# Three settings of a hybrid decoder trunk: which feed-forward chunks use seven products, when a norm is summed, and which engine splits six weight pieces

## The chip, the cores and the metric

The kernel runs on one core of one Trainium2 chip. The metric is the device time of one execution in microseconds (us). The engines are named as in the profile: PE (TensorE), PEld (its weight loads), DVE (VectorE), ACT (ScalarE), POOL (GpSimd) and SP (SyncE, whose queue issues the weight transfers).

## The reference, cut to what matters

A trunk of two layers works on 512 tokens of 1024 features in float32. Each layer has a mixer and then a SwiGLU feed-forward network of 2816 hidden features; layer 0 mixes by attention (a latent group and a differential group), layer 1 by two recurrences.

```python
def swiglu(h, w_gate, w_up, w_down):
    return (jax.nn.silu(h @ w_gate) * (h @ w_up)) @ w_down
...
    x = x + m
    x = x + swiglu(rms_norm(x, norm_ffn[l]), ffn_gate[l], ffn_up[l], ffn_down[l])
```

In the latent group of layer 0 the keys and values come from a normed projection of 256 features:

```python
    kv = (rms_norm(c_kv, kv_norm) @ w_ukv).reshape(bsz, s_len, MLA_HEADS, MLA_NOPE + MLA_V).transpose(0, 2, 1, 3)
```

## The kernel before, in words

**Split products.** Every float32 operand is split into a high and a low part in a format that PE multiplies in one pass; a product of two operands is then three matmuls (`mm3`, L362 to L364): high by high, low by high, high by low. Activations are held as features by tokens in eight tiles of 128x512.

**Weights.** They come from HBM in groups of 512 KB, four of which are held at a time (`NRAW`), and are cut into pieces of 128x512. `cut_one` casts a piece to its high part `wh` on ACT (L300) and subtracts it from the raw weight to get the low part `wl` (L302). The subtraction runs on GpSimd for the pieces numbered `PL[0]` up to `PL[1]`, and on DVE otherwise. The pieces are numbered in the order of use: 0 to 7 are the first projections, 8 to 15 the differential values, 16 to 23 the differential queries and keys of heads 2 and 3, 24 onwards the latent projections. Cutting runs at most eight pieces ahead of use (`NSPL`).

**Steps.** A dense step is one 128x128 weight tile with its three matmuls of 512 columns. After each step `tick` counts one, runs what is due, and may cut a piece. `defer(n, f)` runs `f` n steps later. Instructions go into each engine's queue about in this order, and each queue is worked off in order.

**The feed-forward network.** `ffn` goes through the hidden features in two halves of 11 chunks of 128. A plain chunk has 16 steps, eight for the gate (`pg`) and eight for the up product (`pu`); `gated` then reads both from PSUM (L1092 on DVE, L1093 on ACT, L1094 on DVE, L1095 on GpSimd) and splits the hidden tile (L1096, L1097). PSUM has three banks of the tag `mm` for these: the up product of chunk 3 takes the bank in which the gate product of chunk 2 was. The chunks in `FAST[half]` are computed by `seven` as a Strassen product of 2x2 blocks: seven products of 12 matmuls with 256 columns each (L1054), which need four sums of weights (`combined`, L322 to L330, two on GpSimd and two on DVE) and seven pieces instead of four. They also need four pairs of sums of activations, the same for all such chunks; `halves(j)` makes one pair: two products by the norm's weights on ACT (L1029), four sums on DVE (L1031 to L1034), two casts on ACT (L502) and two subtractions on DVE (L503). Each pair is deferred from the start of chunk 0. The norm's row (`rstd`, L473 to L484) and what is done with chunk 0 come at step 21 (`W0` is 5).

**The latent norm.** In layer 0 a weave of two generators puts attention blocks of the differential heads between dense steps. In `latent_projections`, j counts six tiles of eight steps. The squares of the two key tiles (j of 1 and 2) are added on GpSimd (L517); `scale_kv` sums them over the features with eight matmuls of one column (L683) and takes the root (L687 to L690); `spread_kv` lays the result out over the tokens (L696), loads two tables through SP's queue and turns the shared key (L707 to L711). `SK` gives the steps, counted from j of 3 and j of 4, behind which these two run:

```python
hooks = {3 + SK[0] // 8: {SK[0] % 8: scale_kv}, 4 + SK[1] // 8: {SK[1] % 8: spread_kv}}
```

Of the kernel before, what the change touches and what calls it, by code (L numbers as in the profile page):

```python
# [39 lines left out]
R0, R1 = 8, 12  # L40
W0 = 5
SQ = 2, 6
SK = 2, 0
PT = 2
PL = 16, 72
KP = 4
NW = 16
Z0, Z1 = 3, 9
# [10 lines left out]
HC = lambda nc: nc.scalar.copy  # L59
NSLOT, NTMP, NRAW, NSPL = 38, 10, 4, 8  # L60

FAST = (4, 6, 8, 10), (0, 2, 4, 6, 8, 10)
SEVEN = "a11", "s2", "s1", "a22", "s3", "a12", "s4"


# [117 lines left out]
def drain(gen):  # L183
    for _ in gen:
        pass


class Build:
    def __init__(self, nc, tc, a, ctx, dbg=None):
# [10 lines left out]
        for key, c, src, total, width in self.weight_order():  # L200
            self.chunks[key, c] = len(self.pieces), width
            size = width if key == "first" else 2 * width
            if key[:2] == "gu" and c % HFF in FAST[c // HFF]:
                n = len(self.groups)
# [78 lines left out]
    def cut_one(self):  # L283
# [17 lines left out]
        if lo is not None:  # L301
            (nc.gpsimd if PL[0] <= self.cut < PL[1] else nc.vector).tensor_tensor(out=lo, in0=raw, in1=hi.bitcast(F32), op=ALU.subtract)  # L302
        self.have[self.cut] = hi, lo
# [362 lines left out]
    def latent_projections(self):  # L666
# [56 lines left out]

        hooks = {3 + SK[0] // 8: {SK[0] % 8: scale_kv}, 4 + SK[1] // 8: {SK[1] % 8: spread_kv}}
        for c in range(3):
# [288 lines left out]
    def ffn(self, l, wcol):  # L1014
# [9 lines left out]
        def halves(j):  # L1024

            tt = nc.vector.tensor_tensor
            a, b, s = self.tmp("xa"), self.tmp("xb"), (self.tmp("b12"), self.tmp("b34"))
            for t, k in ((a, j), (b, j + 4)):
                nc.scalar.activation(out=t, in_=self.x[:, k, :], func=AF.Identity, scale=self.par[:, own + k : own + k + 1])  # L1029
            la, lb = slice(0, 256), slice(256, T)  # L1030
            tt(out=s[0][:, la], in0=a[:, lb], in1=a[:, la], op=ALU.subtract)  # L1031
            tt(out=s[0][:, lb], in0=b[:, lb], in1=s[0][:, la], op=ALU.subtract)
            tt(out=s[1][:, la], in0=b[:, lb], in1=a[:, lb], op=ALU.subtract)
            tt(out=s[1][:, lb], in0=s[0][:, lb], in1=b[:, la], op=ALU.subtract)  # L1034
            for i in range(2):
                self.split(mixed[j][0][i], mixed[j][1][i], s[i])

        for half in range(2):
# [50 lines left out]
            def gated(pg, pu, row):  # L1089
                g, u = self.tmp("g"), self.tmp("uu")  # L1090
                h, lo = self.slot("hh", F32R), self.slot("hl", F32R)
                nc.vector.tensor_tensor(out=g, in0=pg, in1=row, op=ALU.mult)  # L1092
                nc.scalar.activation(out=g, in_=g, func=AF.Silu)  # L1093
                nc.vector.tensor_tensor(out=u, in0=pu, in1=row, op=ALU.mult)  # L1094
                nc.gpsimd.tensor_tensor(out=u, in0=u, in1=g, op=ALU.mult)  # L1095
                nc.scalar.copy(out=h, in_=u)  # L1096
                nc.gpsimd.tensor_tensor(out=lo, in0=u, in1=h.bitcast(F32), op=ALU.subtract)  # L1097
                hh.append(h)
                hl.append(lo)

            for m in range(HFF):
                w = self.weights(f"gu{l}", half * HFF + m)
                if half == m == 0:
                    for j in range(KD // 2):
                        self.defer(22 + 7 * j, lambda j=j: halves(j))
                    row = self.first_tiles(w, gated, None, squares)
                    continue
                if m in FAST[half]:
                    seven(w)
                    continue  # L1110
                pg, pu = self.bank("mm"), self.bank("at" if half == 0 and m == 1 else "mm")
                drain(self.featmajor(pg, w, 0, self.ah, self.al))
                drain(self.featmajor(pu, w, 1, self.ah, self.al))
                gated(pg, pu, row)
# [604 lines left out]
```

## Time and profile before

| | us |
|---|---|
| median of 3 runs | 1277.98 (1276.56 to 1280.1) |
| profiled execution | 1278.92 |
| its span | 1277.1 |
| PE busy in it | 1245.8 |

In the profiled execution 1.82 us lie around the span. PE is busy for 98% of the span, and the mean granted clock of TensorE is 0.991 of full speed; a matmul's busy time overlaps with that of the next, so that a stretch is timed by the starts of its matmuls, and an idle PE and a lowered clock are two separate losses.

### The profile page before, as it was taken

Reading aid. Unit: us, or ns where it says so; the run is one execution under the profiler, and the core shown is the slowest. Engines: PE = TensorE matmul, PEld = TensorE weight load, DVE = VectorE, ACT = ScalarE, POOL = GpSimd, SP = SyncE. Lnnn points to the kernel's source line nnn. Section 1 sums busy time; section 2 is a strip of 40 time slices with the busy share of each in tenths; the row PEclk is TensorE's granted clock in tenths of the full one; section 3 lists DMA queues with packets and bytes.
Section 4 is the critical chain, followed back from the end, with each engine's and each line's share of the span. In section 5 each row is a group of like instructions: output and inputs, shape, how many; then the busy total and the mean of one; then the engine's idle time right before and its main releaser. Section 6 shows DMA issues by size and latency. Waiting matters only on the chain.

```text
span 1277.1 us, 18331 instructions
## 1 busy us (share of the span) xinstructions
PE 1245.8 (98%) x6777; PEld 1060.1 (83%) x6777; DVE 845.5 (66%) x1583; ACT 603.4 (47%) x1235; POOL 349.7 (27%) x281
## 2 busy tenths in 40 slices
PE   9999999998999999999999999999989999999997
PEld 7877778876898889898888888777769888999886
DVE  7786676577785456774475466999877744676632
ACT  6555655556444234444433455564554432434441
POOL 0753431123442014331200013210044310335212
PEclk9999999999999999999999999999989999999999
DMA  7222221121323322333422420212313233233321
GB/s 260 87 87 62 83 83 50 34 66 50 100 89 114 110 87 97 101 98 99 130 71 82 133 92 23 70 47 66 94 56 100 79 114 105 85 114 91 107 68 66
DMA packets 38120, 113.37 MB, mean 89 GB/s; under 512 B 4368, under 2 KB 10896, under 8 KB 38032
## 3 DMA queue, kind: packets, MB, share of 16 engines
q1 hardware_dynamic: 37888, 111.95, 28.0%
q8 instruction: 53, 0.87, 0.3%
q14 instruction: 35, 0.29, 0.1%
q10 hardware_dynamic: 144, 0.26, 0.1%
HBM read 110.10 MB, written 2.10 MB: 88 GB/s over the span
## 4 chain that ended last, share of the span: by engine, by line
PE 82%; DVE 7%; ACT 3%; issue 2%; POOL 1%; POOLq 0%; ACTq 0%; DVEq 0%
PE mm L362 18%; PE mm L363 18%; PE mm L364 18%; PE mm L1054 14%; PE at L1054 2%; PE o L947 1%; PE at L781 1%; PE at L1511 1%; DVE bl L503 1%; PE at L903 1%; PE at L800 1%; DVE wl L302 1%; PE o L890 1%; ACT p L792 1%; DVE nm L788 1%
## 5 line engine op out<-in xcount | busy, mean ns | idle before, releaser
L302 DVE TENSOR_TENSOR wl<-wr,wh 128x512 fp32r<-128x512 f32 x332 | 272.7, 831 | 202.9 <-ACT wh L300 200.2
L300 ACT CAST wh<-wr 128x512 fp32r<-128x512 f32 (+1 forms) x385 | 229.7, 608 | 287.8 <-PE mm L363 201.2
L362 PE MATMUL mm<-xh,wh 128*128 128x512 f32 x608 | 242.2, 399 | 9.9 <-DVE g L1092 8.9
L364 PE MATMUL mm<-xh,wl 128*128 128x512 f32 x608 | 240.0, 395 | 0.4 <-POOL wl L302 0.4
L363 PE MATMUL mm<-xl,wh 128*128 128x512 f32 x608 | 239.4, 394 | 0.3 <-DVE xl L506 0.3
L362 PEld LDWEIGHTS mm<-xh,wh 128*128 128x128 f32 x608 | 115.6, 190 | 33.5 <-issue 6.2
L362 PE MATMUL mm<-hh,wh 128*128 128x512 f32 (+1 forms) x363 | 139.2, 383 | 0.0
L363 PE MATMUL mm<-hl,wh 128*128 128x512 f32 (+1 forms) x363 | 138.9, 383 | 0.0
L364 PE MATMUL mm<-hh,wl 128*128 128x512 f32 (+1 forms) x363 | 138.9, 383 | 0.0
L364 PEld LDWEIGHTS mm<-xh,wl 128*128 128x128 f32 x608 | 115.4, 190 | 25.3 <-POOL wl L302 0.9
L363 PEld LDWEIGHTS mm<-xl,wh 128*128 128x128 f32 x608 | 115.8, 190 | 23.3 <-DVE xl L506 0.7
L302 POOL TENSOR_TENSOR wl<-wr,wh 128x512 fp32r<-128x512 f32 (+1 forms) x54 | 69.2, 1288 | 110.3 <-ACT wh L300 103.7
L300 ACT CAST wh<-s 128x512 fp32r<-128x512 f32 x80 | 47.7, 617 | 97.1 <-DVE s L323 71.9
L1095 POOL TENSOR_TENSOR uu<-uu,g 128x512 f32<-128x512 f32 x24 | 42.3, 1764 | 146.4 <-ACT g L1093 68.4
L364 PEld LDWEIGHTS mm<-hh,wl 128*128 128x128 f32 x363 | 68.2, 188 | 13.4
L363 PEld LDWEIGHTS mm<-hl,wh 128*128 128x128 f32 x363 | 68.2, 188 | 13.2
L362 PEld LDWEIGHTS mm<-hh,wh 128*128 128x128 f32 x363 | 68.2, 188 | 13.1
L1083 POOL TENSOR_TENSOR uu<-uu,g 128x512 f32<-128x512 f32 x20 | 30.3, 1515 | 151.7 <-ACT g L1082 151.7
L1054 PE MATMUL mm<-bh,wh 128*128 128x256 f32 x240 | 68.3, 284 | 0.0
L1054 PE MATMUL mm<-xh,wl 128*128 128x256 f32 x240 | 67.9, 283 | 0.0
L1054 PE MATMUL mm<-xl,wh 128*128 128x256 f32 x240 | 67.9, 283 | 0.0
L1054 PE MATMUL mm<-bl,wh 128*128 128x256 f32 x240 | 67.9, 283 | 0.0
(465 smaller groups left out, 2695.4 us busy)
## 6 DMA issues: line engine op xcount, KB each, us to landing
wr<-in_w_gu_dram SPq DMA_DIRECT2D x88, 512.0 KB, 3.6
wr<-in_w_down_dram SPq DMA_DIRECT2D x32, 512.0 KB, 3.5
wr<-in_w_in_dram SPq DMA_DIRECT2D x18, 512.0 KB, 3.7
wr<-in_w_out_dram SPq DMA_DIRECT2D x12, 512.0 KB, 3.5
wr<-in_w_down_dram SPq DMA_DIRECT2D x32, 192.0 KB, 2.4
x<-in_x_dram SPq DMA_DIRECT2D x8, 256.0 KB, 5.8
wr<-in_w_dv_dram SPq DMA_DIRECT2D x4, 512.0 KB, 6.9
tab<-in_con_dram SPq DMA_DIRECT2D x8, 256.0 KB, 4.0
```

What stands on the lines that cost most here:

```text
L300: nc.scalar.copy(out=hi, in_=raw)
L302: (nc.gpsimd if PL[0] <= self.cut < PL[1] else nc.vector).tensor_tensor(out=lo, in0=raw, in1=hi.bitcast(F32), op=ALU.subtract)
L362: mm(out, lh, rh, start=start, stop=False)
L363: mm(out, lh, rl, start=False, stop=False)
L364: mm(out, ll, rh, start=False, stop=stop)
L503: nc.vector.tensor_tensor(out=lo, in0=src, in1=hi.bitcast(F32), op=ALU.subtract)
L781: nc.tensor.matmul(s[:, 0:n], qb, k[:, 0:n], start=True, stop=True)
L788: nc.vector.tensor_reduce(out=nm, in_=s[:, 0:n], axis=AX.X, op=ALU.max, negate=True)
L792: nc.scalar.activation(out=pt[:, 0:n], in_=s[:, 0:n], func=AF.Exp, bias=nm, accum_out=rsum)
L1054: mm = lambda x, y, a, b: nc.tensor.matmul(ps[:, la], x, y, start=a, stop=b, skip_group_check=True)
L1083: nc.gpsimd.tensor_tensor(out=u, in0=u, in1=g, op=ALU.mult)
L1095: nc.gpsimd.tensor_tensor(out=u, in0=u, in1=g, op=ALU.mult)
```

## The change

`FAST[0]`, the chunks of the first half that use seven products, becomes 5, 7 and 9 in place of 4, 6, 8 and 10, in both layers; the second half stays. The four pairs of sums of activations are deferred by 38, 47, 56 and 65 steps in place of 22, 29, 36 and 43. `scale_kv` and `spread_kv` run three dense steps later. Pieces 16 to 21 have their low part subtracted on DVE in place of GpSimd.

```diff
-SK = 2, 0
+SK = 5, 3
 PT = 2
-PL = 16, 72
+PL = 22, 72
...
-FAST = (4, 6, 8, 10), (0, 2, 4, 6, 8, 10)
+FAST = (5, 7, 9), (0, 2, 4, 6, 8, 10)
...
                 if half == m == 0:
                     for j in range(KD // 2):
-                        self.defer(22 + 7 * j, lambda j=j: halves(j))
+                        self.defer(38 + 9 * j, lambda j=j: halves(j))
```

## Rows read from the trace of the kernel before

**Rows 1.** The page's first part: busy us, share of span, instructions.

```profile
PE 1245.8 (98%) x6777; PEld 1060.1 (83%) x6777; DVE 845.5 (66%) x1583; ACT 603.4 (47%) x1235; POOL 349.7 (27%) x281
```

**Rows 2.** PE's waits by releaser: us in total, times, longest.

```profile
PE mm L362 <- DVE g L1092: 8.9, 2, 5.8
```

**Rows 3.** Windows of layer 0's chunks: length, PE, PEld, DVE, ACT, POOL busy, clock, DMA.

```profile
296.73:307.61 10.88, 10.88 (x49) 9.01 (x48) 10.26 (x19) 8.24 (x14) 4.77 (x3) 1.00 0.02 3
307.61:313.05 5.44, 5.44 (x25) 4.32 (x23) 3.08 (x5) 3.01 (x6) 4.81 (x4) 1.00 0.24 90
313.05:319.03 5.98, 0.16 (x1) 0.03 (x1) 5.98 (x11) 2.80 (x6) 0.94 (x1) 0.76 0.00 0
319.03:326.45 7.42, 7.42 (x25) 5.94 (x26) 6.31 (x7) 3.44 (x7) 3.15 (x2) 0.73 0.41 116
326.45:336.55 10.10, 10.10 (x86) 10.10 (x85) 7.24 (x10) 3.94 (x8) 6.30 (x4) 1.00 0.28 78
336.55:347.45 10.90, 10.90 (x51) 9.01 (x50) 8.12 (x14) 5.10 (x9) 2.90 (x2) 1.00 0.35 106
```

**Rows 4.** Windows of layer 1: chunk 3 between its two products, and its second.

```profile
943.58:948.96 5.38, 0.55 (x2) 0.19 (x2) 5.38 (x10) 3.10 (x7) 1.63 (x1) 0.88 0.00 0
948.96:957.09 8.13, 8.13 (x24) 6.51 (x25) 5.52 (x8) 3.34 (x7) 4.69 (x2) 0.66 0.37 129
```

**Rows 5.** Timeline of DVE in layer 0's chunks 2 and 3: start us, us.

```profile
306.36 0.41 DVE L1033 TENSOR_TENSOR b<-xb,xa 128x256 f32<-128x256 f32 x1
...
310.40 1.85 DVE L503 TENSOR_TENSOR bl<-b,bh 128x512 fp32r<-128x512 f32 x1 [2.36 <-ACT bh L502]
...
317.60 0.68 DVE L503 TENSOR_TENSOR bl<-b,bh 128x512 fp32r<-128x512 f32 x1
318.21 0.68 DVE L1092 TENSOR_TENSOR g<-mm,row 128x512 f32<-128x512 f32 x1
```

**Rows 6.** Timeline of POOL and ACT there.

```profile
305.65 3.55 POOL L1095 TENSOR_TENSOR uu<-uu,g 128x512 f32<-128x512 f32 x1 [5.38 <-ACT xa L1029]
...
309.23 0.62 ACT L1096 CAST hh<-uu 128x512 fp32r<-128x512 f32 x1 [2.98 <-POOL uu L1095]
```

**Rows 7.** Timeline of PE, POOL and DVE around pieces 16 to 23.

```profile
53.08 0.50 PE L364 MATMUL mm<-xh,wl 128*128 128x512 f32 x1 [0.43 <-POOL wl L302]
...
51.75 8.76 POOL L302 TENSOR_TENSOR wl<-wr,wh 128x512 fp32r<-128x512 f32 x7
...
56.69 3.85 DVE L918 SCALAR_TENSOR_TENSOR ri<-ri,nlam,rsa 128x1 f32<-128x1 f32 x1
...
63.32 0.22 DVE L918 SCALAR_TENSOR_TENSOR ri<-ri,nlam,rsa 128x1 f32<-128x1 f32 x1
```

**Rows 8.** Timelines of PE and DVE: scores of the fourth block, their maximum, a later wait.

```profile
71.82 0.22 PE L904 MATMUL at<-mqb,identb 128*128 128x128 bf16 x1
...
73.11 1.28 DVE L788 TENSOR_REDUCE nm<-at 128x1 f32<-128x512 f32 x2
...
89.33 1.16 PE L890 MATMUL o<-dv,pT 128*128 128x128 f32 x8 [1.65 <-ACT pT L803]
```

**Rows 9.** Timelines of PE and DVE around the latent keys' norm.

```profile
109.21 1.05 PE L683 MATMUL at<-con,acck 128*128 128x1 f32 x8 [1.06 <-POOL acck L517]
...
113.33 0.16 DVE L690 SCALAR_TENSOR_TENSOR lr<-lr,rs 128x4 f32<-128x4 f32 x1
...
118.59 1.05 PE L696 MATMUL at<-con,lr 128*128 128x128 f32 x8
```

**Rows 10.** Windows behind the two one-column sums, of keys and of queries.

```profile
110.00:112.00 2.00, 2.00 (x11) 1.69 (x11) 0.71 (x3) 0.89 (x3) 0.77 (x2) 0.85 0.28 76
112.00:114.00 2.00, 2.00 (x10) 1.63 (x9) 1.38 (x4) 0.00 (x0) 0.88 (x1) 0.50 0.24 73
114.00:116.00 2.00, 2.00 (x14) 1.69 (x13) 0.85 (x2) 1.26 (x5) 0.00 (x0) 0.80 0.96 296
...
138.00:140.00 2.00, 1.66 (x11) 1.38 (x11) 1.93 (x6) 0.32 (x2) 0.50 (x1) 1.00 0.85 272
```

## The prediction

> **What bounds the kernel now.** I read the page's busy times first: PE is busy for 98% of the span [rows 1], so only two things can shorten the kernel by much, less work for PE or fewer stretches in which PE stands or runs slowly. DVE and ACT have room on average; what they cost is where PE waits for them. The list of PE's waits says where that is: one pair is far above the rest, the first matmul of a product waiting for DVE's read of a gate bank, 8.9 us in two places [rows 2].
>
> The windows then show those places. In layer 0, chunk 2 and the gate product of chunk 3 run at the full pace: 10.88 us for 16 steps and 5.44 us for eight, 0.68 us a step. Then PE stands for 5.98 us, and the next eight steps take 7.42 us instead of 5.44, because the granted clock is 0.73 in that stretch [rows 3]: TensorE fell from 2.4 GHz to 1.2 GHz while it stood and came back some microseconds later. Layer 1 has the same: 5.38 us and then 8.13 us [rows 4]. The reader should see that the lowered clock is a second loss behind each wait, a third to a half of its size.
>
> Why DVE is late is in the timelines. The gate product of chunk 2 was ready half a chunk after 296.73, but DVE reads it at 318.21; the up product of chunk 3 needs that bank at 313.05 [rows 3, 5]. Before it in DVE's queue stand the four pairs of activation sums. DVE is busy for 10.26 us of chunk 2's 10.88 [rows 3], and in between it also idles 2.36 us for a cast [rows 5]. That cast stands on ACT behind the cast of a hidden tile, which waited 2.98 us for a GpSimd product that took 3.55 us [rows 6]. So it is a backlog of several in-order queues, and it is full just when the bank is wanted.
>
> **The sums made later.** By work a pair of sums costs DVE four operations of 0.41 us and two of 0.68 us, 3.0 us [rows 5]; the pairs now start at steps 22, 29, 36 and 43, which is chunks 1 and 2, and the norm's row arrives at step 21 with five more DVE operations. At 38, 47, 56 and 65 two pairs fall into chunk 2, one into chunk 3 and one into chunk 4, all plain. Between the norm's row and chunk 2's gate read two pairs, 6.0 us of DVE work, are gone, and the read was late by 318.21 + 0.68 - 313.05 = 5.8 us [rows 3, 5]. With the first seven-product chunk moved to 5, its extra pieces and its DVE sum move out of chunk 2 too, and the slowed operations (1.85 us where 0.68 us is usual, [rows 5]) with them. Chunk 2 then holds two pairs, four splits and two reads by `gated`, 6.0 + 6 x 0.68 = 10.1 us by these durations against 10.88: tight, but without the debt from chunk 1. The second pair, of step 47, is the only one directly ahead of the critical read. Its step is at 47 x 0.68 on the steps' own clock, two steps ahead of chunk 3, and the bank is wanted eight steps into chunk 3: 10 x 0.68 = 6.8 us for a pair of 3.0 us with its casts. I take the wait as gone in both layers. Bounds: nothing gained, or all of it. All of it is 5.98 + (7.42 - 5.44) = 7.96 us in layer 0 and 5.38 + (8.13 - 5.44) = 8.07 us in layer 1: **-16.03 us**.
>
> What is late next: the first seven-product chunk needs all four pairs from its second product on. In layer 0 the last subtraction of the fourth pair ended at 317.60 + 0.68 = 318.28, while its step 43, ten steps into chunk 2, was at 296.73 + 6.80 = 303.53: 14.75 us [rows 3, 5]. After the change there are 16 steps and one product (12 of 84 matmuls, 1.44 us of 10.10, [rows 3]) between step 65 and that need, 12.3 us. As slow as before it would cost 2.4 us a layer; without the debt I count nothing, and carry 4.9 us as a bound.
>
> **One chunk fewer in seven products.** A seven-product chunk takes 10.10 us and a plain one 10.90 us [rows 3]. One is exchanged in each layer: **+1.60 us**, on PE's path, certain. It also takes seven splits down to four and the four weight sums away, off the path.
>
> **Six splits on DVE.** GpSimd subtracts seven pieces in a train of 8.76 us; PE waits 0.43 us for the first [rows 7]. DVE does one in 0.68 us for a tile of that size [rows 5] and stands idle when this one is ready: **-0.43 us**, bounds 0 and 0.43. The six on DVE, 4.1 us, run beside ACT's casts; DVE's next need is for ACT's exponentials, which stand behind the same casts, so I count nothing for them, with 0.5 us as a bound. The train had a second price: a DVE operation on single columns took 3.85 us beside it and 0.22 us alone [rows 7]. That puts DVE 3.6 us behind, but by the fourth block's scores most is made up: they end at 72.04 and their maximum starts at 73.11, 1.07 us late [rows 8]. At 89.33 PE waits 1.65 us for a transposed block on ACT [rows 8]. I take 1.1 us of it, the lateness that a chain caught up with PE can still lose; bounds 0 and 1.65: **-1.1 us**. GpSimd gives up 7.5 us of work (6 x 1.25, from the train), and its queue behind gets earlier.
>
> **The keys' norm three steps later.** PE stands 1.06 us before the one-column sums, for GpSimd's sum of squares [rows 9]. Three steps are 2.04 us, and an attention block lies in between as well: **-1.06 us**, with nothing as the other bound. Behind the wait the granted clock is 0.85, 0.50 and 0.80 in three windows of 2 us [rows 10], a loss of 0.30 + 1.00 + 0.40 = 1.70 us; behind the same eight matmuls for the queries the clock stayed at 1.00 [rows 10]. I take it back: **-1.70 us**, bounds 0 and 1.70. The spreading moves by as much, but the attention block that stood between the two is no longer there: from the sums' start to DVE's last step takes 113.33 + 0.16 - 109.21 = 4.28 us, and the room falls from 118.59 - 109.21 = 9.38 us to the sums and six steps, 0.91 + 6 x 0.71 = 5.2 us (0.71 being the step beside attention, an estimate from 118.59 back over four steps) [rows 9]. If the block's own cast and subtraction, some 1.4 us, stand ahead of it on DVE and ACT, PE waits 0.5 us; I count nothing. The two table loads of the spreading go through SP's queue three steps later, ahead of weights that are eight pieces from their use.
>
> **Sum.** -16.03 + 1.60 - 0.43 - 1.1 - 1.06 - 1.70 = -18.72 us. The profiled execution took 1278.92, 0.94 above the median; 1278.92 - 18.72 = 1260.2, and against the median 1277.98 - 18.7 = **1259.3 us**.
>
> **The rivals.** A measurement of this kernel tells about 0.3%, 3.8 us, from no change.
>
> The clock falls all the same behind the keys' sums. For it: after the move these eight one-column matmuls stand one step behind a block of masks and transposes, all short matmuls, and only the wait is gone. Against it: the queries' sums, with 0.34 us of waiting, left the clock at 1.00 [rows 10]. Time: 1259.3 + 1.7 = 1261.0. The Trainium skill has a rule that speaks for it: "TensorE: Matmul & The Clock Gate", Part 4, says that transposes do not count as PE-busy for the clock as other matmuls do. By that rule the time would be 1261.0; the queries' window does not show it.
>
> One of the two waits stays, or half of each: chunk 2 is tight by the sum above, and 4.9 us of the fourth pair are in the bounds. Time: 1259.3 + 8.0 = 1267.3.
>
> Both waits stay whole, a chunk later: the queues' debt comes from the casts behind GpSimd's product [rows 6], which remain, and not from the pairs. Then only attention and the exchange are left, 18.7 - 16.0 = 2.7 us gained: 1275.3, no change by the bound.
>
> Slower: the fourth pair holds up the first seven-product chunk. Each microsecond past 12.3 costs one in each layer; to be 0.3% slower it must eat 18.7 + 3.8 = 22.5 us, 11.3 us a layer, so the pair would have to end 23.6 us after its step, where it ended after 14.75 under the heavier load: 1282 or more.
>
> **How the numbers follow.** The forecast as it stands has 0.62, the falling clock 0.13, one wait left 0.15, both left 0.07, slower 0.03. The range goes from 1256.5, the forecast less the rest of the 1.65 us and 2.2 us of scatter (the three runs lie within 2.1 us of their median), to 1268.5, which takes in the third case. Faster has 0.62 + 0.13 + 0.15 = 0.90, no change 0.07, slower 0.03.
>
> **What would show it.** Right: in both layers the wait of the up product for the gate's read is gone from PE's list, chunks 2 to 4 follow each other every 10.9 us at a clock of 1.00, and the first seven-product chunk starts without a wait. Six low parts of pieces 16 to 21 stand on DVE, and the column operation after them takes 0.2 us. No wait is left before the keys' sums, and the clock is 1.00 behind them. Wrong: PE waits in chunk 3 or 4 for a gate's read, or in chunk 5 for a sum's subtraction; PE waits before the spreading; the wait for a transposed block is as long as before.

## The result, and the profile after

| us | before | after |
|---|---|---|
| median, timed side by side | 1278.81 (4 runs, 1276.56 to 1280.1) | 1264.48 (4 runs, 1263.25 to 1265.0) |
| profiled execution's span | 1277.1 | 1261.5 |
| mean granted clock | 0.991 | 0.997 |

The ratio is 0.9888 with a 95% interval of 0.9871 to 0.9906: 14.3 us faster, where 18.7 were forecast.

The first part of the page after, to be laid beside [rows 1], shows PE 6.1 us less busy, and 74 matmuls fewer in the records (the exchange is 2 x (84 - 48) = 72 of them); the rest of the 15.6 us between the spans, 9.5 us, is time in which PE no longer stands.

```profile
PE 1239.7 (98%) x6703; PEld 1053.2 (83%) x6705; DVE 834.6 (66%) x1567; ACT 598.6 (47%) x1225; POOL 333.7 (26%) x271
```

PE's waits after (total, times, longest): the 8.9 us for the gate's read that led the list in [rows 2] are gone. At the top stands a wait that was not in the list of before, for DVE's sum `uv` of a seven-product chunk (L1064), and third is another new one, for the keys' norm before its spreading.

```profile
PE mm L1054 <- DVE uv L1064: 2.6, 2, 1.5
PE at L1609 <- DVE frs L461: 1.9, 1, 1.9
PE at L696 <- DVE lr L690: 1.3, 2, 1.1
...
PE o L890 <- ACT pT L803: 0.3, 1, 0.3
```

The windows of layer 0's chunks 2, 3, 4, 5 and 6, and of layer 1's chunk 5 (length; PE, PEld, DVE, ACT, POOL busy; clock; DMA), answer to [rows 3, 4]:

```profile
291.63:302.51 10.88, 10.88 (x49) 9.01 (x48) 8.86 (x16) 8.07 (x15) 5.84 (x4) 1.00 0.22 55
302.51:313.39 10.88, 10.88 (x50) 9.01 (x48) 10.88 (x15) 5.81 (x11) 4.47 (x3) 1.00 0.29 91
313.39:324.27 10.88, 10.88 (x50) 9.01 (x48) 10.21 (x14) 5.79 (x11) 4.46 (x3) 1.00 0.15 49
324.27:335.65 11.38, 10.32 (x85) 10.12 (x84) 8.05 (x12) 4.69 (x10) 6.29 (x4) 1.00 0.35 97
335.65:346.56 10.91, 10.91 (x50) 9.02 (x49) 8.18 (x14) 5.10 (x9) 2.92 (x2) 1.00 0.33 102
948.88:960.74 11.86, 10.35 (x86) 10.14 (x85) 8.53 (x13) 4.90 (x10) 6.28 (x4) 1.00 0.31 92
```

Three plain chunks in a row take 10.88 us each at a clock of 1.00, where chunk 3 alone took 5.44 + 5.98 + 7.42 = 18.84 us before. The first seven-product chunk takes 11.38 us in layer 0 and 11.86 us in layer 1 instead of 10.10: the new wait. The timeline of that chunk, from PE, DVE, GpSimd and ACT in turn (start us, us, engine, line; what ended the idle time in brackets), says what PE waits for:

```profile
331.24 0.39 PE L1054 MATMUL mm<-bh,wh 128*128 128x256 f32 x1 [1.05 <-DVE uv L1064]
...
956.32 0.39 PE L1054 MATMUL mm<-bh,wh 128*128 128x256 f32 x1 [1.51 <-DVE uv L1064]
...
325.84 0.68 DVE L1094 TENSOR_TENSOR uu<-mm,row 128x512 f32<-128x512 f32 x1
...
329.75 1.10 DVE L302 TENSOR_TENSOR wl<-wr,wh 128x512 fp32r<-128x512 f32 x1 [2.63 <-ACT wh L300]
330.77 0.41 DVE L1064 TENSOR_TENSOR uv<-mm,pp 128x256 f32<-128x256 f32 x1
...
326.67 1.60 POOL L1095 TENSOR_TENSOR uu<-uu,g 128x512 f32<-128x512 f32 x1 [6.33 <-DVE uu L1094]
...
328.30 0.62 ACT L1096 CAST hh<-uu 128x512 fp32r<-128x512 f32 x1 [2.58 <-POOL uu L1095]
328.83 0.37 ACT L1062 COPY pp<-mm 128x256 f32<-128x256 f32 x1
```

The fifth product of the chunk takes the bank of the second and so waits for L1064. That sum needs ACT's copy of the first product (L1062), and the copy stands on ACT behind the cast of chunk 4's hidden tile, for which ACT idled 2.58 us until GpSimd had its product of 1.60 us. Behind the copy stands a weight's cast, on which DVE idled 2.63 us with the sum queued behind it. It is the same in-order chain as in [rows 6], with another victim.

### The profile page after: what moved, and what is told of

Read it like the earlier page. It is cut to its first block, busy times and chain, and to the rows that moved or that the text cites. A ratio compares the mean times of both kernels' runs of the same rounds, so it can differ in the third digit from the quotient of the medians.

```text
span 1261.5 us, 18137 instructions
## 1 busy us (share of the span) xinstructions
PE 1239.7 (98%) x6703; PEld 1053.2 (83%) x6705; DVE 834.6 (66%) x1567; ACT 598.6 (47%) x1225; POOL 333.7 (26%) x271
## 4 chain that ended last, share of the span: by engine, by line
PE 88%; DVE 7%; ACT 3%; issue 2%; POOL 1%; DMA 0%; POOLq 0%; SPq 0%; ACTq 0%; DVEq 0%
PE mm L362 21%; PE mm L363 20%; PE mm L364 20%; PE mm L1054 12%; PE at L1054 2%; PE o L947 1%; PE at L903 1%; PE at L781 1%; PE at L800 1%; PE at L1511 1%; PE at L362 1%; PE at L363 1%; PE at L364 1%; DVE wl L302 1%; ACT p L792 1%
## 5 line engine op out<-in xcount | busy, mean ns | idle before, releaser
L302 DVE TENSOR_TENSOR wl<-wr,wh 128x512 fp32r<-128x512 f32 (+1 forms) x340 | 272.7, 812 | 204.2 <-ACT wh L300 201.4
L362 PE MATMUL mm<-xh,wh 128*128 128x512 f32 x640 | 251.9, 394 | 1.2 <-ACT xh L505 1.2
L364 PE MATMUL mm<-xh,wl 128*128 128x512 f32 x640 | 250.1, 391 | 0.0
L363 PE MATMUL mm<-xl,wh 128*128 128x512 f32 x640 | 249.7, 390 | 0.3 <-DVE xl L506 0.3
L364 PEld LDWEIGHTS mm<-xh,wl 128*128 128x128 f32 x640 | 120.2, 188 | 25.0
L302 POOL TENSOR_TENSOR wl<-wr,wh 128x512 fp32r<-128x512 f32 (+1 forms) x48 | 61.7, 1288 | 113.8 <-ACT wh L300 105.7
L363 PEld LDWEIGHTS mm<-hl,wh 128*128 128x128 f32 x363 | 68.2, 188 | 13.3
L364 PEld LDWEIGHTS mm<-hh,wl 128*128 128x128 f32 x363 | 68.2, 188 | 13.2
L1054 PE MATMUL mm<-bh,wh 128*128 128x256 f32 x216 | 61.6, 285 | 2.6 <-DVE uv L1064 2.6
L1054 PE MATMUL mm<-xh,wl 128*128 128x256 f32 x216 | 61.1, 283 | 0.0
L1054 PE MATMUL mm<-xl,wh 128*128 128x256 f32 x216 | 61.1, 283 | 0.0
L1054 PE MATMUL mm<-bh,wl 128*128 128x256 f32 x216 | 61.1, 283 | 0.0
```

The source lines that it names most:

```text
L362: mm(out, lh, rh, start=start, stop=False)
L363: mm(out, lh, rl, start=False, stop=False)
L364: mm(out, ll, rh, start=False, stop=stop)
L1054: mm = lambda x, y, a, b: nc.tensor.matmul(ps[:, la], x, y, start=a, stop=b, skip_group_check=True)
```

## The experiments

Each edit is made to the kernel before, unless it says "to the kernel after"; ratios are to the kernel before, timed on the same chip.

**The attention part and the feed-forward part apart.** The first:

```diff
-SK = 2, 0
+SK = 5, 3
-PL = 16, 72
+PL = 22, 72
```

> The kernel before with the two attention edits alone (pieces 16 to 21 split on DVE, the keys' norm three steps later). If the parts of the change add up, about 5 us below before (1273 to 1274.5), with the seven-product waits of both layers as in before. If instead the early gain is used up by a later wait in the same layer, within 2 us of before.

Measured: 1275.70 against 1277.46, ratio 0.9984 (0.9974 to 0.9993). That is 1.8 us, not the 5 that was expected first but the other case, "within 2 us of before". The second has the other two settings:

```diff
-FAST = (4, 6, 8, 10), (0, 2, 4, 6, 8, 10)
+FAST = (5, 7, 9), (0, 2, 4, 6, 8, 10)
...
-                        self.defer(22 + 7 * j, lambda j=j: halves(j))
+                        self.defer(38 + 9 * j, lambda j=j: halves(j))
```

> The kernel before with the feed-forward edits alone (chunks 5, 7, 9 and pairs at 38 + 9 j). If the parts add up, about 11 us below before (1266.5 to 1269): both waits for the gate's read gone, 1.6 us paid for the plain chunks, and 1.0 and 1.5 us waited inside the first seven-product chunk. If the attention edits are what gave DVE its room there, less than 6 us below.

Measured: 1266.00 against 1277.46, ratio 0.9906 (0.9886 to 0.9925), 11.5 us. The parts add up, 1.8 + 11.5 = 13.3 against 14.3 for both.

**Which of the two settings of the feed-forward part.** The chunks alone, and a deferral alone, by 30, 39, 48 and 57 steps, so that all pairs start ahead of chunk 4, which stays in seven products:

```diff
-FAST = (4, 6, 8, 10), (0, 2, 4, 6, 8, 10)
+FAST = (5, 7, 9), (0, 2, 4, 6, 8, 10)
```

> Only the seven-product chunks moved to 5, 7, 9; the pairs of sums stay at 22 + 7 j. If the pairs behind the norm's row are the debt (the prediction's theory), a wait for the gate's read of 3 us or more stays in chunk 3 of each layer with its lowered clock, and the time is 1270 to 1277. If the weight sums and extra pieces of the first seven-product chunk were the debt, the waits are gone and the time is 1264 to 1267.

```diff
-                        self.defer(22 + 7 * j, lambda j=j: halves(j))
+                        self.defer(30 + 9 * j, lambda j=j: halves(j))
```

> Only the pairs moved, to 30 + 9 j (the last must stand before chunk 4); chunks 4, 6, 8, 10 keep seven products. If the pairs behind the norm's row are the debt, the gate's wait in chunk 3 shrinks by half or more, but the fourth pair then stands 6 us ahead of its need and holds up chunk 4 by 2 to 6 us a layer: 1266 to 1274. If the weight sums were the debt, within 3 us of before.

Measured: 1275.42, ratio 0.9988 (0.9974 to 1.0002), and 1274.81, ratio 0.9982 (0.9972 to 0.9991). Neither alone is worth 3 us; together they are worth 11.5. The first lies in the range expected for it, the second 0.8 us above its range. The timeline of PE with the chunks alone still has a wait of some 4 us in each layer before chunk 3's up product, in layer 1 put down to a cast of the pairs:

```profile
314.46 0.47 PE L362 MATMUL mm<-xh,wh 128*128 128x512 f32 x1 [4.16 <-DVE g L1092]
...
943.25 0.74 PE L362 MATMUL mm<-xh,wh 128*128 128x512 f32 x1 [3.64 <-ACT bh L502]
```

With the deferral alone, PE's list of waits shows them one chunk later, in the seven-product chunk 4, for chunk 3's gate read:

```profile
PE mm L1054 <- DVE g L1092: 6.7, 2, 3.7
```

What holds chunk 4 is thus a gate's read and not, as was expected, the fourth pair. By the starts of PE's rows, the way from the norm's row (L473) to the first seven-product chunk is shorter than before by 6.25 and 7.35 us, and the way from there to the next one longer by 5.35 and 6.51 us. So the third rival of the prediction, a debt that only moves, is what happens when the pairs move without the chunks: as these two runs read, the pairs need plain chunks around them, and the first seven-product chunk has to stay clear of them.

**What holds the fifth product.** If it is the chain behind GpSimd's product, that product on DVE for chunk 4 alone takes the wait away. To the kernel after:

```diff
-            def gated(pg, pu, row):
+            def gated(pg, pu, row, first=False):
...
-                nc.gpsimd.tensor_tensor(out=u, in0=u, in1=g, op=ALU.mult)
+                (nc.vector if first else nc.gpsimd).tensor_tensor(out=u, in0=u, in1=g, op=ALU.mult)
...
-                gated(pg, pu, row)
+                gated(pg, pu, row, half == 0 and m == 4)
```

> The changed kernel with one edit: the hidden product of chunk 4 of the first half runs on DVE (about 0.7 us) and not on GpSimd (1.6 us). If the first seven-product chunk waits because ACT's copy and casts stand behind the cast of chunk 4's hidden tile, which waits for GpSimd, the waits of 1.05 and 1.51 us for DVE's sum L1064 shrink to under 0.5 us each and the time falls by 1 to 2.6 us against the changed kernel. If DVE is simply full there, the added DVE work leaves the waits as long or makes them longer.

Its rival is that the pairs, now late, hold DVE. Then earlier pairs take it away. To the kernel after:

```diff
-                        self.defer(38 + 9 * j, lambda j=j: halves(j))
+                        self.defer(34 + 9 * j, lambda j=j: halves(j))
```

> The changed kernel with the pairs four steps earlier, 34 + 9 j. If the fourth pair's collision with GpSimd's three operations at a chunk's end is what makes DVE late at chunk 4's end, a shift moves the operations off that train and the waits inside the first seven-product chunk change by more than 0.5 us a layer. If it is only the order on ACT's queue, they stay at 1.0 and 1.5 us. A gate's wait in chunk 3 may come back by up to 2 us a layer if chunk 2 is as tight as the prediction had it.

Measured: 1261.50, ratio 0.9877 (0.9862 to 0.9892), against 1264.38, ratio 0.9901 (0.9886 to 0.9915). With the product on DVE the wait has left the list. In the timeline of that kernel the copy now goes ahead of the cast, and in the window the chunk takes 10.10 us:

```profile
328.02 0.37 ACT L1062 COPY pp<-mm 128x256 f32<-128x256 f32 x1
329.49 0.62 ACT L1096 CAST hh<-uu 128x512 fp32r<-128x512 f32 x1 [1.10 <-DVE uu L1095]
...
328.76 0.69 DVE L1095 TENSOR_TENSOR uu<-uu,g 128x512 f32<-128x512 f32 x1
```

```profile
325.98:336.08 10.10, 10.10 (x86) 10.09 (x85) 9.12 (x12) 4.91 (x10) 4.70 (x3) 1.00 0.44 133
```

With pairs four steps earlier the wait stays, and no wait for a gate's read comes back:

```profile
PE mm L1054 <- DVE uv L1064: 2.4, 2, 1.3
```

The two waits are 1.31 and 1.08 us there, where they were 1.05 and 1.51: neither changed by more than 0.5 us. That speaks for the queues' order and, as far as a shift by four steps can tell, against the place of the pairs.

**The attention part taken apart.** Six splits on DVE alone, and the norm's move alone:

```diff
-PL = 16, 72
+PL = 22, 72
```

> The kernel before with only the six splits on DVE. Measured on the stretch from the first scores to the first latent values, 137.2 us in the three profiles with before's attention and no lowered clock, 135.6 with both edits. If the splits bring all of the gain and the keys' norm nothing (a wait of 1.1 us goes, one of 1.1 to 1.4 us comes), 135.3 to 136.0. If the norm's move brings its 1.06 us, 136.4 or more.

```diff
-SK = 2, 0
+SK = 5, 3
```

> The kernel before with only the keys' norm three steps later. If the wait before the spreading takes the place of the one before the sums, the stretch stays near 137.2 us (136.8 to 137.7). If the prediction's 1.06 us is won, 136.2 or less.

Measured: 1274.65 and 1279.39 in one execution each, against a median of 1277.69 (1275.89 to 1281.08), and stretches of 136.78 and 138.56 us, both longer than expected. By the words of the expectation the first of them, above 136.4, would even speak for the norm's move. In the second profile the wait for GpSimd's first low part was 1.08 us, where [rows 7] have 0.43. One execution is too little for such sizes, so I take the same two stretches from all profiles, by the starts of PE's rows. From the first matmul of L903 (51.36 us in the profile before) to the product that waited 1.65 us in [rows 8]: with GpSimd's splits 37.97 us before and 37.04 to 38.91 in four others, a mean of 37.93; with the splits on DVE 35.69 to 37.12 in eight profiles, a mean of 36.1; the two ranges just overlap. From there to the first matmul of L947, the first latent values (190.65 us in the profile before): 101.32 us before, 99.62 of it without the 1.70 us of the lowered clock, and 99.65 to 99.67 in four others with the norm's old place; 99.62 to 99.89 in six with the new one. The splits bring about 1.8 us, and the norm's move brings nothing where the clock is not lowered. Two rows of PE's timeline with the norm's move alone show why: the wait before the sums is gone, and one of 1.13 us stands before the spreading.

```profile
113.96 0.95 PE L683 MATMUL at<-con,acck 128*128 128x1 f32 x8
...
121.64 1.13 PE L696 MATMUL at<-con,lr 128*128 128x128 f32 x8 [1.13 <-DVE lr L690]
```

Would more distance between the two help? To the kernel after, the spreading three further steps later:

```diff
-SK = 5, 3
+SK = 5, 6
```

> The changed kernel with the spreading of the keys' norm another three steps later (5, 6). If PE's new wait of 1.13 us before the spreading is only DVE's chain being too close, it goes: the stretch from the first scores to the first latent values falls from 135.6 to about 134.5 us, and the time by about 1 us. If a later wait takes its place, the stretch stays.

Measured: 1265.51, ratio 0.9907 (0.9892 to 0.9922), no better than the kernel after, with a stretch of 138.6 us. The wait before the spreading is gone, but the sums of the queries, which wait 0.34 us in the kernel before, now wait 2.0 us for GpSimd, and behind them the windows show a lowered clock. All four executions have it, with a mean granted clock of 0.995 or 0.996 where the kernel after has 0.997.

```profile
134.00:136.00 2.00, 2.00 (x10) 1.90 (x11) 1.97 (x6) 0.95 (x5) 0.00 (x0) 0.57 0.91 287
136.00:138.00 2.00, 2.00 (x6) 1.53 (x5) 1.05 (x6) 1.15 (x6) 0.00 (x0) 0.50 0.83 274
138.00:140.00 2.00, 2.00 (x6) 1.60 (x5) 0.65 (x4) 0.61 (x3) 0.00 (x0) 0.50 0.09 33
140.00:142.00 2.00, 2.00 (x12) 1.77 (x12) 0.00 (x0) 0.97 (x4) 0.60 (x1) 0.73 0.00 0
```

**A fourth seven-product chunk.** The exchange of a chunk costs 0.8 us a layer; chunk 10 gives it back without touching the start. To the kernel after:

```diff
-FAST = (5, 7, 9), (0, 2, 4, 6, 8, 10)
+FAST = (5, 7, 9, 10), (0, 2, 4, 6, 8, 10)
```

> The changed kernel with a fourth seven-product chunk again, 5, 7, 9 and 10. If PE's columns are what bounds the half, 0.8 us less in each layer, 1.6 us below the changed kernel. If two seven-product chunks in a row need more splits and sums than DVE and ACT can do in 20 us, PE waits in chunk 10 and the time is the same or higher.

Measured: 1263.47, ratio 0.9892 (0.9875 to 0.9908). From the norm's row (L473) to the second half's first seven-product chunk the two layers got shorter by 0.17 and 0.24 us, not 0.8; two more waits for the same sum, 2.9 - 2.6 = 0.3 us in all, explain a part, and the rest was not settled.

**A version from what was found.** The product of chunk 4 on DVE, and the keys' sums one step earlier than in the kernel after, so that their chain has a step more of room. To the kernel with the product on DVE:

```diff
-SK = 5, 3
+SK = 4, 3
```

> The changed kernel with chunk 4's hidden product on DVE and the keys' sums one step earlier (4, 3), so that they stand ahead of the attention block and the spreading stays behind it. If the waits are as read, both the 2.8 us in the feed-forward layers and the 1.1 us before the spreading go: the stretch is 134.3 to 134.8 us and the time 1259.5 to 1261.5. If GpSimd's sum of squares is not ready there, PE waits before the sums by up to 0.7 us and the stretch is 135 or more.

Measured: 1260.17 (1257.99 to 1260.5) against 1277.69, ratio 0.9858 (0.9836 to 0.988); the stretch is 134.2 us. In its timeline neither the sums nor the spreading wait. All four executions are shorter than those of the kernel after (1263.25 to 1265.0), but the two were not timed side by side, and the intervals of their ratios overlap.

```profile
107.50 0.95 PE L683 MATMUL at<-con,acck 128*128 128x1 f32 x8
...
115.77 1.05 PE L696 MATMUL at<-con,lr 128*128 128x128 f32 x8
```

## Why the prediction was right, and where its sum was off

The direction, the place and the main term were right; 4.4 us of 18.7 did not come.

| step | forecast | measured |
|---|---|---|
| waits for the gate's read, with the clock | -16.03 | -16.03 |
| one seven-product chunk fewer a layer | +1.60 | +1.60 |
| what is late next in the feed-forward part | 0 | +3.07 |
| six splits on DVE, both prices | -1.53 | -1.8 |
| wait before the keys' sums | -1.06 | 0.0 |
| lowered clock behind them | -1.70 | 0 |
| sum | -18.72 | -13.2 |

The measured sum lies within the interval of the ratio, which is 12.0 to 16.5 us. One of the prediction's own signs of being wrong came: PE waits before the spreading.

The two profiled executions differ by 15.6 us in their spans. By the starts of PE's rows 1.39 us of it lie ahead of the first scores, 2.09 + 1.63 between them and the first latent values, and 5.85 + 5.49 in the first halves of the feed-forward parts. At the end the kernel after loses 0.94 us: its last eight matmuls (L1609) take 2.08 us at a granted clock of 0.50, where they took 1.16 us before at 1.00. The prediction has no term for that. From L1609 on, the nine profiles with an edit of the feed-forward part need 7.1 to 7.7 us and the four without one 6.7 to 6.8; the cause stays open.

**The main term** came out as worked: the way from the norm's row (L473) to the first seven-product chunk is 37.70 and 37.58 us before, 40.62 and 40.39 after. That is one plain chunk of 10.88 us more, less 7.96 and 8.07: the two losses of [rows 3, 4], whole. In layer 0 the read of chunk 2's gate ended at 302.36 + 0.68 = 303.04, and its bank was wanted at 302.51 + 5.44 = 307.95: 4.9 us to spare, so it was no luck. DVE's timeline after, with the fourth pair's last subtraction below it:

```profile
302.36 0.68 DVE L1092 TENSOR_TENSOR g<-mm,row 128x512 f32<-128x512 f32 x1
...
322.68 0.68 DVE L503 TENSOR_TENSOR bl<-b,bh 128x512 fp32r<-128x512 f32 x1
```

The place of "tight" was wrong: DVE is busy for 8.86 us of chunk 2 and for all 10.88 us of chunk 3. A pair cost 3.0 us only without a GpSimd operation beside it; in chunks 3 and 4 three of its sums took 1.5 us instead of 0.41, so the slowed operations had not gone, as the prediction had it, but moved along. The exchange costs its 0.8 us a layer.

**"What is late next"** is the first step that failed. I looked for it at the fourth pair, wanted at the second product, with 4.9 us as its bound and nothing counted. The pair was in time: its last subtraction ended at 322.68 + 0.68 = 323.36, ahead of the chunk's start at 324.27. (The step counts there are one too many, 14.75 and 12.3 us are 14.07 and 11.6, which leaves their difference as it is.) Late was a sum that I had not followed at all, L1064, wanted at the fifth product: from the first seven-product chunk to the next takes 22.29 and 22.76 us where 20.99 is usual, a loss of 1.30 + 1.77 = 3.07 us. The prediction named the cause itself, casts behind GpSimd's product, in its third rival, but priced it only where it already hurt. The experiment with that product on DVE returned the loss but for 0.33 us in layer 1, which was not followed: 20.98 and 21.32 us.

**The keys' norm** is the second. "4.28 us" from the sums' start to DVE's last step was carried over unchanged to a place where other work stands on the same queues. The timeline of DVE after shows the chain of [rows 9] there:

```profile
110.84 0.73 DVE L506 SCALAR_TENSOR_TENSOR dl<-at,sub,dh 128x512 fp32r<-128x512 f32 x1
111.49 0.16 DVE L688 TENSOR_SCALAR lv<-lv 128x4 f32<-128x4 f32 x1
113.11 0.75 DVE L506 SCALAR_TENSOR_TENSOR cql<-mm,par,cqh 128x512 fp32r<-128x512 f32 x1 [1.46 <-ACT cqh L505]
113.77 0.54 DVE L459 TENSOR_TENSOR ll<-lr 128x4 f32<-128x4 f32 x1
...
116.51 0.16 DVE L690 SCALAR_TENSOR_TENSOR lr<-lr,rs 128x4 f32<-128x4 f32 x1
```

From the sums' start at 109.15 it now takes 116.51 + 0.16 - 109.15 = 7.5 us: the attention block's subtraction, the low part of a projection with its 1.46 us for a cast, and the spreading's own table products stand between the steps. The room had been estimated at 5.2 us and is 116.82 - 1.13 - 109.15 = 6.5 us; 1.13 us of waiting came for the 1.06 that went. The text saw "0.5 us" of it and counted nothing.

**The lowered clock** is the third, and the fault is one of reading. The loss of 1.70 us was real in the profile before, but four profiles of kernels that kept the norm's place, with the same wait of 1.05 to 1.07 us before the same sums, have the clock at 1.00 from 106 to 126 us. Of these the second window of [rows 10] in the kernel with the feed-forward edits alone, and below it the same window of the kernel after:

```profile
112.00:114.00 2.00, 2.00 (x16) 1.72 (x14) 1.43 (x6) 0.73 (x3) 0.26 (x1) 1.00 0.31 32
...
112.00:114.00 2.00, 2.00 (x11) 1.64 (x10) 0.90 (x2) 1.17 (x4) 1.97 (x2) 1.00 0.08 31
```

How often it comes is not settled. The profiled execution, which the prediction itself had put 0.94 us above the median, has a mean granted clock of 0.991; of the 39 executions of the kernel before that were timed beside the experiments 12 have 0.991 or less, with a mean of 1278.4 us against 1276.9 for the rest. That would fit such a loss in about a third of them, but no profile shows where they lost it. None of the ten executions with both attention edits is below 0.992, so the norm's move may save it where it comes; no run separates that. A loss that most executions do not have cannot be taken off the median. Its rival, "the clock falls all the same", fell too: all windows from 108 to 118 us after are at 1.00, where the sums stand one step behind an attention block. The rule of the Trainium skill ("TensorE: Matmul & The Clock Gate", Part 4) that transposes do not count as PE-busy in the same way did not show there.

**The splits** were right: their low parts stand on DVE as a train, and the column operation behind it takes its 0.22 us [rows 7]. The wait for the transposed block went from 1.65 to 0.26 us [rows 8].

```profile
50.08 3.70 DVE L302 TENSOR_TENSOR wl<-wr,wh 128x512 fp32r<-128x512 f32 x6 [1.98 <-ACT wh L300]
55.53 0.22 DVE L918 SCALAR_TENSOR_TENSOR ri<-ri,nlam,rsa 128x1 f32<-128x1 f32 x1
...
85.85 1.16 PE L890 MATMUL o<-dv,pT 128*128 128x128 f32 x8 [0.26 <-ACT pT L803]
```

## What to carry to other kernels

When a wait is taken away, follow the delayed work queue by queue to the next instruction that PE needs; look first at whatever stood behind the same blocking instruction, since the block itself (a cast waiting for another engine's product) is still there. A chain of small operations has no fixed length: price it with the neighbours it will have on each queue at its new place. And before a dip of the clock is counted as a gain, see in how many executions it is.

## What the runs showed of the hardware that was not expected

DVE's small operations stretch to the length of GpSimd's. In chunk 4 of the kernel after, three sums that take 0.41 us alone [rows 5] took 1.5 us each, side by side with three GpSimd operations of 1.60, 1.48 and 1.47 us; the next sum, after the last of those, took 0.41 us. Each of the three ended 0.27 to 0.28 us after the GpSimd operation beside it, and the price of each turn is 1.1 us.

```profile
316.24 1.51 DVE L1031 TENSOR_TENSOR b<-xa 128x256 f32<-128x256 f32 x1
317.68 1.51 DVE L1033 TENSOR_TENSOR b<-xb,xa 128x256 f32<-128x256 f32 x1
319.11 1.50 DVE L1032 TENSOR_TENSOR b<-xb,b 128x256 f32<-128x256 f32 x1
...
321.14 0.41 DVE L1034 TENSOR_TENSOR b<-b,xb 128x256 f32<-128x256 f32 x1
...
315.87 1.60 POOL L1095 TENSOR_TENSOR uu<-uu,g 128x512 f32<-128x512 f32 x1 [6.33 <-DVE uu L1094]
317.43 1.48 POOL L327 TENSOR_TENSOR s<-wr,wr 128x512 f32<-128x512 f32 x1
318.87 1.47 POOL L1097 TENSOR_TENSOR hl<-uu,hh 128x512 fp32r<-128x512 f32 x1
```

The Trainium skill ("SBUF — State Buffer", "SBUF: two separate sides") says that a DVE operation with two inputs in SBUF and a GpSimd operation that reads SBUF take a shared pair of ports from each other for a whole instruction; these rows agree. In [rows 7] one turn was not enough: the column operation, begun at 56.69, ended at 60.54, 0.03 us after GpSimd's train at 51.75 + 8.76 = 60.51, so it waited for some three subtractions. Why it got no turn between them is not shown.

A wait of about 1 us does not settle the clock: of the profiles with 1.05 to 1.07 us before the keys' sums one lost 1.70 us to it and four nothing, the waits of 1.05 and 1.51 us in the first seven-product chunk left it at 1.00, and 2.0 us before the queries' sums lost 0.86 + 1.00 + 1.00 + 0.54 = 3.4 us by the windows above.

The kernel's first matmuls run at half their pace for longer in some executions than in others, whatever the kernel: 0.43 us from start to start where 0.23 is usual. Two timelines of PE, of the kernel after and of the one with the deferral alone, with a window of the second:

```profile
5.55 0.73 PE L362 MATMUL mm<-xh,wh 128*128 128x512 f32 x2 [1.22 <-ACT xh L505]
...
7.06 0.40 PE L364 MATMUL mm<-xh,wl 128*128 128x512 f32 x1
```

```profile
5.39 1.22 PE L362 MATMUL mm<-xh,wh 128*128 128x512 f32 x2 [0.74 <-ACT xh L505]
...
7.68 0.63 PE L364 MATMUL mm<-xh,wl 128*128 128x512 f32 x1
```

```profile
6.00:8.00 2.00, 2.00 (x6) 1.61 (x5) 1.27 (x3) 1.10 (x3) 0.00 (x0) 1.00 0.99 338
```

The granted clock reads 1.00 in that window, so these rows do not say what slows the matmuls.

The first L903 starts at 49.8 to 50.0 us or at 51.3 to 51.9 us by it, so that two profiles differ by up to 2 us before the code does; 1.39 us of the difference between the spans of before and after is this.
